# dt from split operands, the context convolution in the first half, a wider-spaced scan, and latent kernels expanded on ScalarE

## The chip, the cores and the metric

One core of a Trainium2 chip runs the whole program as one launch. The metric is the device time of that launch in microseconds (us), lower is better; it is given as the median of repeated runs. The engines are TensorE (PE, with its weight loads PEld), VectorE (DVE), ScalarE (ACT), GpSimd (POOL) and SyncE (SP), which here only issues DMAs. Everything is stored and returned in float32.

## What is computed

One layer of a backbone is applied to 256 context tokens and 2048 latent tokens (a grid of 32 rows by 64 columns), width 1024. Every token is normalised and modulated, projected by one input matrix, passed through two branches, and projected back:

```python
h = rms_norm(x, g_pre) * (1 + scale) + shift
u = h @ w_in
z, xbc, dt_raw, ga, gb, gsil = jnp.split(u, [I_Z, I_XBC, I_DT, I_GA, I_GB], axis=-1)
y_ssd, h_fin = ssd_branch(z, xbc, dt_raw, ...)
y_conf = conformer_branch(ga, gb, ...)        # h = ga*sigmoid(gb); depthwise 31-tap conv; layer_norm; silu
out = jnp.concatenate([y_ssd, y_conf * jax.nn.silu(gsil)], axis=-1) @ w_out
return x + gate * rms_norm(out, g_post), h_fin
```

`ssd_branch` is a Mamba-2 scan in both directions over chunks of 128 tokens: a 5-tap convolution of `xbc`, step sizes `dt = softplus(dt_raw + bias)` (32 columns: 16 heads in two directions), and per chunk a part inside the chunk, a part from the carried state and the new state. In `conformer_branch` the 31 taps run along the context's tokens, and along the rows of the latent grid.

## The kernel before

Tokens are cut into five blocks: block 0 is the context (256 tokens), blocks 1 to 4 are 512 latent tokens each. **Half 0** works on blocks 1, 2, 0, **half 1** on blocks 3 and 4. PSUM has 3 banks for the projections (tag "mm") and 5 for all else (tag "ss").

**Blocks.** `hprep(b)` normalises and modulates a block in eight pieces `ht` of 128 channels and splits each into a high and a low part, `hh` and `hl`, in the type f32r (L283 and L284). A projection runs as three f32r matmuls for each piece, hh·wh (L350), hl·wh (L351), hh·wl (L352): a unit of 24 matmuls fills a bank of 512 tokens. `dt_raw` alone is computed in plain f32, in `split` of `hprep`: one matmul per piece (L282) with 32 weight columns, written to one of four strips of 32 partitions, k % 4. The strips are copied (L300), transposed and added up (L307); `dt_post` makes the scan's factors out of the result.

**Stages.** `xbc_phase` projects `xbc` (banks xp) and starts the 5-tap convolution (`cva`, DVE L447 and L451). `post` then runs 8 `gab_unit`s (banks gb and ga; ACT and DVE make `gth` of them, L501 and L504, which goes to the DRAM buffer `gl`, L505) and 13 or 14 `silu_unit`s (banks sp; `sth`, L514 and L515). In half 0 the scan of chunks 0 to 8 and `gate_rows` run beside `post`, in half 1 the scan of chunks 9 to 17 with `lat_conv` and `ctx_conv`. Last comes the output stage (L1037).

**The scan.** `pass_a(i)` takes one chunk through eleven steps, for two groups g of 8 heads and two directions d. `weigh(g, d)` makes `xw` (DVE L675), its high part `xwh` (ACT L676) and its low part `xwl` (L677, on DVE for d = 1, on POOL for d = 0); `state(g, d)` multiplies them in three matmuls into `pst` (L699, L700, L701); `diag` makes `py`, `off` makes `po`; `carry(g)` puts `po` away as `yo` (DVE L707) and adds `pst` to the running state `Sf` (DVE L709). `state` runs one step after the `weigh` that feeds it, and a new chunk starts each six steps.

**The convolutions.** `ctx_conv(j)` loads 128 channels of the context from `gl` (L549) and runs 31 taps on DVE into the tile `cg` (one L553, 30 L555), then transposes and stores them. `lat_conv(j)` loads the filter rows `kd` and the latent channels `cx`, and four times `expand(u)` writes a block matrix into one of two tiles `kbuf` (L590: 8 copies of 32 partitions x 128, half on DVE, half on ACT), with which PE convolves (banks cp, L601); DVE adds the bias (`cvv`, L606).

**Order.** The generators are stepped against each other by `merge` and `interleave`; a scheduler then orders each engine's instructions by its own estimate, with semaphores between engines. Each engine runs its list in that order. All DMAs are issued by SP, in order.

## Time and profile before

| | |
|---|---|
| median of 3 runs | 1910.53 us (1909.71 to 1910.89) |
| the profiled execution's own time | 1917.09 us |
| its span in the trace | 1915.4 us, mean granted clock 0.986 |
| busy: PE, DVE, ACT, POOL | 1853.9, 1183.0, 786.2, 643.8 us |
| DMA | 375.30 MB, 62.8% of the 16 engines' span |

In time: 0 to 60 us startup, 60 to 200 xbc of half 0, 200 to 770 `post` of half 0, 770 to 950 its last `silu_unit`s, the blocks 3 and 4 and xbc of half 1, 950 to 1460 `post` of half 1, 1460 to the end the output stage. A row of waits names the engine that waits, what for, and the total, the number and the longest. A row of the timeline has start, length, engine, line, operation, tiles and, in brackets, the idle time before it.

### The profile page before, as it was taken

How to read it: one execution, taken by the hardware profiler on the slowest of the kernel's cores; microseconds unless marked ns; L12 is line 12 of the kernel's file. 1: busy time of each engine (PE TensorE's matmuls, PEld its weight loads, DVE VectorE, ACT ScalarE, POOL GpSimd, SP SyncE). 2: the span in 40 equal slices, each digit the busy share in tenths (PEclk: the TensorE clock that was granted, in tenths of full speed). 3: DMA queues.
4: the chain of work that ended last, by engine and by line, in shares of the span. 5: the costliest groups of instructions: out<-in, count | busy, mean ns of one | idle time of the engine just before them, and what ended most of it. 6: DMA issues, size and time to landing. Idle time of an engine off the chain costs nothing.

```text
span 1915.4 us, 27056 instructions
## 1 busy us (share of the span) xinstructions
PE 1853.9 (97%) x9739; PEld 1492.7 (78%) x9739; DVE 1183.0 (62%) x1603; ACT 786.2 (41%) x1746; POOL 643.8 (34%) x612
## 2 busy tenths in 40 slices
PE   7999899999999999999999899989999999999998
PEld 4588778888888878588877667767787888888886
DVE  3687774333344442678597778889437767766752
ACT  3445524444444542346335655555314332222321
POOL 2533423444544432402133343333115322332220
...
GB/s 311 194 189 186 204 220 183 182 219 163 219 218 207 196 230 203 140 160 185 187 180 196 227 238 209 230 216 210 221 264 235 207 165 171 177 172 166 180 99 77
DMA packets 290386, 375.30 MB, mean 196 GB/s; under 512 B 85190, under 2 KB 187462, under 8 KB 290252
## 3 DMA queue, kind: packets, MB, share of 16 engines
q1 hardware_dynamic: 290252, 373.58, 62.8%
...
## 4 chain that ended last, share of the span: by engine, by line
PE 66%; DVE 7%; issue 6%; DMA 3%; POOL 2%; ACT 2%; SPq 0%; POOLq 0%; DVEq 0%
PE op L1037 19%; PE sp L350 6%; PE sp L351 6%; PE sp L352 6%; DVE cg L555 3%; PE xp L350 2%; PE xp L352 2%; PE xp L351 2%; PE gb L350 2%; PE gb L351 2%; PE gb L352 2%; PE ga L350 2%; PE ga L351 2%; PE ga L352 2%; PE qo L944 1%
## 5 line engine op out<-in xcount | busy, mean ns | idle before, releaser
L350 PE MATMUL sp<-hh,wh 128*128 128x512 f32 (+1 forms) x640 | 241.1, 377 | 0.0
L351 PE MATMUL sp<-hl,wh 128*128 128x512 f32 (+1 forms) x640 | 237.3, 371 | 0.0
L352 PE MATMUL sp<-hh,wl 128*128 128x512 f32 (+1 forms) x640 | 236.9, 370 | 0.0
L650 ACT ACTIVATE lb<-lb,WB 128x128 f32<-128x128 f32 x576 | 181.5, 392 | 98.5 <-POOL lb L642 97.1
L350 PE MATMUL xp<-hh,wh 128*128 128x512 f32 (+1 forms) x480 | 181.3, 378 | 8.0 <-ACT raw L435 7.3
L642 POOL TENSOR_SCALAR_AFFINE_SELECT lb<-lb 128x512 f32<-128x512 f32 x144 | 118.9, 833 | 202.3 <-DMA lb<-lt 124.9
L352 PE MATMUL xp<-hh,wl 128*128 128x512 f32 (+1 forms) x480 | 179.6, 375 | 0.6 <-POOL wl L326 0.6
L351 PE MATMUL xp<-hl,wh 128*128 128x512 f32 (+1 forms) x480 | 180.1, 376 | 0.0
L447 DVE SCALAR_TENSOR_TENSOR cva<-raw,cwh,cva 128x1280 f32<-128x1280 f32 (+1 forms) x96 | 154.3, 1612 | 33.5 <-ACT cva L441 31.5
L326 POOL TENSOR_TENSOR wl<-wr,wh 128x512 fp32r<-128x512 f32 x88 | 131.4, 1506 | 122.4 <-ACT wh L325 112.6
L350 PEld LDWEIGHTS sp<-hh,wh 128*128 128x128 f32 x640 | 121.2, 189 | 27.0 <-issue 7.3
L555 DVE SCALAR_TENSOR_TENSOR cg<-cg,cv 128x256 f32<-128x256 f32 x240 | 138.8, 591 | 3.6
L351 PEld LDWEIGHTS sp<-hl,wh 128*128 128x128 f32 x640 | 121.4, 190 | 21.3 <-issue 1.7
L352 PEld LDWEIGHTS sp<-hh,wl 128*128 128x128 f32 x640 | 121.0, 189 | 21.7 <-issue 0.8
L350 PE MATMUL ga<-hh,wh 128*128 128x512 f32 (+1 forms) x320 | 121.3, 379 | 5.8 <-DMA wh<-whd 5.6
L350 PE MATMUL gb<-hh,wh 128*128 128x512 f32 (+1 forms) x320 | 122.3, 382 | 4.5 <-DVE gth L504 4.5
L515 DVE SCALAR_TENSOR_TENSOR sth<-sth,sp 128x512 f32<-128x512 f32 (+1 forms) x80 | 50.3, 631 | 120.8 <-ACT sth L514 116.0
L351 PE MATMUL gb<-hl,wh 128*128 128x512 f32 (+1 forms) x320 | 120.1, 375 | 0.0
L352 PE MATMUL gb<-hh,wl 128*128 128x512 f32 (+1 forms) x320 | 120.0, 375 | 0.0
L351 PE MATMUL ga<-hl,wh 128*128 128x512 f32 (+1 forms) x320 | 119.2, 372 | 0.0
L352 PE MATMUL ga<-hh,wl 128*128 128x512 f32 (+1 forms) x320 | 119.1, 372 | 0.0
L350 PEld LDWEIGHTS xp<-hh,wh 128*128 128x128 f32 x480 | 92.0, 192 | 31.8 <-ACT raw L435 7.9
(218 smaller groups left out, 4033.1 us busy)
## 6 DMA issues: line engine op xcount, KB each, us to landing
lb<-lt SPq DMA_DIRECT2D x144, 256.0 KB, 4.4
wr<-in_w_in SPq DMA_DIRECT2D x88, 256.0 KB, 4.3
...
yp<-yg SPq DMA_DIRECT2D x36, 256.0 KB, 4.4
```

Of the source, the lines that this page charges most:

```text
L326: G.tensor_tensor(wl[:, ks, :], wr, wh[:, ks, :].bitcast(F32), SUB)
L350: T.matmul(ps[:, :BN], wh[:, k, :], hh[:, k, :], start=(k == 0), stop=False)
L351: T.matmul(ps[:, :BN], wh[:, k, :], hl[:, k, :], start=False, stop=False)
L352: T.matmul(ps[:, :BN], wl[:, k, :], hh[:, k, :], start=False, stop=(k == KT - 1))
L447: V.scalar_tensor_tensor(a[:, :n], raw[:, t:t + n], cwh[:, ct * 5 + t:ct * 5 + t + 1], a[:, :n], MUL, ADD)
L515: V.scalar_tensor_tensor(th, th, 1.0, ps[:, :BN], ADD, MUL)
L555: V.scalar_tensor_tensor(acc, g[:, t:t + 256], cv[:, w0 + t:w0 + t + 1], acc, MUL, ADD)
L642: G.affine_select(E[g, hq, d], E[g, hq, d], pattern=[[0, 4], [sg, P]], compare_op=ALU.is_ge, fill=NEG, base=0, channel_multiplier=-sg)
L650: S.activation(lb[:, h, :], lb[:, h, :], AF.Exp, bias=WB[:, i, c + h:c + h + 1])
L944: T.matmul(po[:, q * P:(q + 1) * P], Sb[g][:, q * P:(q + 1) * P], ct[:, g, :], start=True, stop=True)
L1037: T.matmul(pso[n], lhs[:, k % 8, :], w[:, n * 512:(n + 1) * 512], start=(k == 0 and m == 0), stop=(k == 15 and m == 2))
```

## The change

1. **dt.** The f32 matmuls leave `split`. A new generator `dt_block` runs, for each of the eight pieces, two f32r matmuls (L315 with `hh`, L316 with `hl`) with 128 weight columns, of which 32 are the high and 32 the low part of w_dt (the rest belongs to the next piece and is not used); the first two strips are added up. `xbc_phase` steps it between the projections. `w_dt` is split on DVE once.
2. **The context convolution** moves from half 1 to half 0, behind `gate_rows`, takes its tiles from the pool "x4" (three buffers, shared with `gate_rows`), and hands over after every 3 taps rather than 6.
3. **The scan.** `weigh` and `mix` come a step earlier against `diag` and `state`, so `state` runs two steps after its `weigh`; `xwh` and `xwl` have two buffers, `el` is two tiles, and chunks start each seven steps.
4. **The latent kernels** are expanded by 4 ACT copies of 32 x 256 rather than 4 ACT and 4 DVE copies of 32 x 128.
5. `dynamic_dma_scratch_size` is 512 rather than 1024, and one tile of modulation weights is loaded in two DMAs.


```diff
@@ dt: hprep (split), new dt_block, its weights @@
-            q = k % 4
-            T.matmul(pd[q * 32:(q + 1) * 32, :BN], wdt[:, k, :], t, start=(k < 4), stop=(k >= 4))
...
+    def dt_block(b, hb):
...
+        for k in range(KT):
+            w = wdt[:, k * 64:k * 64 + P]
+            T.matmul(pd[:, :BN], w, hh[:, k, :], start=(k == 0), stop=False)
+            T.matmul(pd[:, :BN], w, hl[:, k, :], start=False, stop=(k == KT - 1))
+            if k % 2:
+                yield
...
+    V.tensor_copy(wd4[:, :, 0, :], wdr)
+    V.tensor_tensor(wd4[:, :, 1, :], wdr, wd4[:, :, 0, :].bitcast(F32), SUB)
@@ xbc_phase @@
+                    if s > 10 and s % 2 and dts:
+                        next(dts[0], None)
...
-            if m % (14, 9)[half] == 4:
+            if m % 8 == 4:
                 next(dtp, None)
@@ ctx_conv @@
-        g = lp.tile([P, D], F32, tag="cg", name=f"cg{j}", bufs=2)
+        g = big(f"cg{j}")
...
-            if t % 6 == 0:
+            if t % 3 == 0:
                 yield
@@ lat_conv, expand(u) @@
-                src = kd[rs].rearrange("p r (h u q) -> u p h q r", h=2, u=4)[u]
-                for h in range(2):
-                    eng = S.copy if c4 % 2 else V.tensor_copy
-                    eng(kt[rs, h * 4:(h + 1) * 4, rs], src[:, h])
+                S.copy(kt[rs, :, rs].rearrange("p (h q) r -> p h q r", h=2),
+                       kd[rs].rearrange("p r (h u q) -> p u h q r", h=2, u=4)[:, u])
@@ pass_a: buffers and order of a chunk @@
-            el = pa.tile([P, 8, P], F32, tag="el", name=f"el{i}", bufs=1)
+            for g in range(2):
+                el[g] = pa.tile([P, 4, P], F32, tag=f"el{g}", name=f"el{i}{g}", bufs=1)
...
-            wh = pa.tile([P, 512], F32R, tag="xwh", name=f"xwh{i}{g}{d}", bufs=1)
-            wl = pa.tile([P, 512], F32R, tag="xwl", name=f"xwl{i}{g}{d}", bufs=1)
+            wh = pa.tile([P, 512], F32R, tag="xwh", name=f"xwh{i}{g}{d}", bufs=2)
+            wl = pa.tile([P, 512], F32R, tag="xwl", name=f"xwl{i}{g}{d}", bufs=2)
...
-        diag(0, 0)
-        off(0)
-        state(0, 0)
         weigh(0, 1)
         mix(0, 1)
...
+        diag(0, 0)
+        off(0)
+        state(0, 0)
+        weigh(1, 0)
+        mix(1, 0)
...
         diag(0, 1)
         state(0, 1)
         carry(0)
-        weigh(1, 0)
-        mix(1, 0)
-        decay(1, 1)
+        weigh(1, 1)
+        mix(1, 1)
@@ scan @@
-            if gens and t % 6 == 0:
+            if gens and t % 7 == 0:
@@ main sequence @@
-    interleave(post(0, 6), merge(scan(range(9)), 58, gate_rows(), 9), 90 * 8)
+    extra = chain([gate_rows()] + [ctx_conv(j) for j in range(8)])
+    interleave(post(0, 6), merge(scan(range(9)), 68, extra, 9 + 8 * 13), 90 * 8)
...
-    extra = chain(f for j in range(8) for f in (lat_conv(j, lp, kbuf), ctx_conv(j, lp)))
+    extra = chain([lat_conv(j, lp, kbuf) for j in range(8)])
...
-    interleave(take(blocks, 344), merge(sc_, 54, extra, 8 * 13), 344)
+    interleave(take(blocks, 344), merge(sc_, 63, extra, 8 * 6), 344)
...
-    nc = _bacc.Bacc("TRN2", target_bir_lowering=False, num_devices=1, dynamic_dma_scratch_size=1024)
+    nc = _bacc.Bacc("TRN2", target_bir_lowering=False, num_devices=1, dynamic_dma_scratch_size=512)
```

**PE, dt of block 3** (`pd3` is its bank of dt, `sp0_4640_...` the last silu units of half 0, `xp1_...` the xbc projection of half 1). Before:

```order
L282 MATMUL pd3_6974<-ht3_0_6975,wdt_251 32x512
L350 MATMUL sp0_4640_7_2_7009<-hh2_655,wh5536_0_6748 128x512
L282 MATMUL pd3_6974<-ht3_1_6985,wdt_251 32x512
L351 MATMUL sp0_4640_7_2_7009<-hl2_656,wh5536_0_6748 128x512
L352 MATMUL sp0_4640_7_2_7009<-hh2_655,wl5536_0_6747 128x512
L282 MATMUL pd3_6974<-ht3_2_6998,wdt_251 32x512
L350 MATMUL sp0_4640_7_2_7009<-hh2_655,wh5536_0_6748 128x512
L351 MATMUL sp0_4640_7_2_7009<-hl2_656,wh5536_0_6748 128x512
L352 MATMUL sp0_4640_7_2_7009<-hh2_655,wl5536_0_6747 128x512
L282 MATMUL pd3_6974<-ht3_3_7016,wdt_251 32x512
```

and with the change:

```order
L315 MATMUL pd3_7605<-hh3_7291,wdt_252 128x512
L316 MATMUL pd3_7605<-hl3_7292,wdt_252 128x512
L370 MATMUL xp1_1_3_7583<-hh3_7291,wh1152_1_7252 128x512
L371 MATMUL xp1_1_3_7583<-hl3_7292,wh1152_1_7252 128x512
L372 MATMUL xp1_1_3_7583<-hh3_7291,wl1152_1_7251 128x512
L370 MATMUL xp1_1_3_7583<-hh3_7291,wh1152_1_7252 128x512
L371 MATMUL xp1_1_3_7583<-hl3_7292,wh1152_1_7252 128x512
L372 MATMUL xp1_1_3_7583<-hh3_7291,wl1152_1_7251 128x512
L315 MATMUL pd3_7605<-hh3_7291,wdt_252 128x512
L316 MATMUL pd3_7605<-hl3_7292,wdt_252 128x512
L315 MATMUL pd3_7605<-hh3_7291,wdt_252 128x512
L316 MATMUL pd3_7605<-hl3_7292,wdt_252 128x512
```

The eight f32 matmuls stood one by one among the f32r matmuls of the silu units; sixteen f32r matmuls now stand in pairs and fours among those of the next phase.

**DVE, the taps and `xwl` of chunk 14 in half 1** (`kbuf`, `cvv`: latent convolution; `xwl1401` is the low part for g = 0, d = 1). Before:

```order
L555 SCALAR_TENSOR_TENSOR cg5_11421<-cg5_11421,cv_214 128x256 x2
L590 COPY kbuf1_8122<-kd4_10614 32x4x32
L606 SCALAR_TENSOR_TENSOR cvv4_10624<-cp4_1_10710,cbb4_10611 128x16x32
L590 COPY kbuf1_8122<-kd4_10614 32x4x32 x3
L555 SCALAR_TENSOR_TENSOR cg5_11421<-cg5_11421,cv_214 128x256 x5
L707 TENSOR_TENSOR yo140_10834<-po140_10741,el14_10399 128x512
L555 SCALAR_TENSOR_TENSOR cg5_11421<-cg5_11421,cv_214 128x256
L709 TENSOR_TENSOR Sf0_256<-Sf0_256,pst1400_10746 128x512
L677 TENSOR_TENSOR xwl1401_10752<-xw1401_10750,xwh1401_10751 128x512
```

and with the change:

```order
L701 TENSOR_TENSOR xw1401_10835<-xt140_10721,WS_256 128x512
L631 SCALAR_TENSOR_TENSOR cvv3_10366<-cp3_3_10761,cbb3_10353 128x16x32
L680 TENSOR_TENSOR lb14110_10810<-lb14110_10810,lb14111_10812 128x512
L703 TENSOR_TENSOR xwl1401_10837<-xw1401_10835,xwh1401_10836 128x512
L681 TENSOR_TENSOR lb14110_10810<-lb14110_10810,cb14_10717 128x512
L531 SCALAR_TENSOR_TENSOR gth1_7_3_10700<-gth1_7_3_10700,ga1_7_3_10702 128x512
L701 TENSOR_TENSOR xw1410_10910<-xt141_10790,WS_256 128x512
L733 TENSOR_TENSOR yo140_10944<-po140_10901,el140_10562 128x512
L735 TENSOR_TENSOR Sf0_258<-Sf0_258,pst1400_10906 128x512
```

No tap of the context is left among them, and `xwl1401` stands ahead of the `yo` and `Sf` of its chunk.

**DVE, the gates of half 0** (`gth0_j_b` is gate unit j of block b; `cg2` takes its data from what `gth0_2_0` stored). Before:

```order
L504 SCALAR_TENSOR_TENSOR gth0_2_0_2853<-gth0_2_0_2853,ga0_2_0_2855 128x256
L675 TENSOR_TENSOR xw110_2980<-xt11_2808,WS_254 128x512
L727 TENSOR_TENSOR yg10_2826<-yg10_2826,py10_2868 128x512
L675 TENSOR_TENSOR xw111_3095<-xt11_2808,WS_254 128x512
L504 SCALAR_TENSOR_TENSOR gth0_3_1_3008<-gth0_3_1_3008,ga0_3_1_3010 128x512
L707 TENSOR_TENSOR yo11_3154<-po11_3086,el1_2496 128x512
L709 TENSOR_TENSOR Sf1_257<-Sf1_257,pst110_3091 128x512
L677 TENSOR_TENSOR xwl111_3097<-xw111_3095,xwh111_3096 128x512
```

and with the change:

```order
L531 SCALAR_TENSOR_TENSOR gth0_2_0_3006<-gth0_2_0_3006,ga0_2_0_3008 128x256
L701 TENSOR_TENSOR xw111_3133<-xt11_2890,WS_256 128x512
L680 TENSOR_TENSOR lb2000_3197<-lb2000_3197,lb2001_3199 128x512
L580 TENSOR_SCALAR cg2_3586<-cg2_3586,cv_214,cfb2_249 128x256
L582 SCALAR_TENSOR_TENSOR cg2_3586<-cg2_3586,cv_214 128x256
L753 TENSOR_TENSOR yg10_2908<-yg10_2908,py10_3021 128x512
L582 SCALAR_TENSOR_TENSOR cg2_3586<-cg2_3586,cv_214 128x256 x2
L703 TENSOR_TENSOR xwl111_3135<-xw111_3133,xwh111_3134 128x512
L582 SCALAR_TENSOR_TENSOR cg2_3586<-cg2_3586,cv_214 128x256 x7
L531 SCALAR_TENSOR_TENSOR gth0_3_1_3147<-gth0_3_1_3147,ga0_3_1_3149 128x512
L582 SCALAR_TENSOR_TENSOR cg2_3586<-cg2_3586,cv_214 128x256
L680 TENSOR_TENSOR lb2010_3279<-lb2010_3279,lb2011_3281 128x512
```

Taps now stand between the gates; the first instruction on `cg2` comes three places behind the gate `gth0_2_0` whose stored result it loads. Up to `gth0_3_2` there follow 30 taps, `yg` twice, `lb` five times, and one each of `xwl`, `gth0_3_1`, `yo`, `Sf`, `btl` and `xw`.

## Rows read from the trace of the kernel before

**Rows 1.** The page's first part: busy us and share of the span.
```profile
PE 1853.9 (97%) x9739; PEld 1492.7 (78%) x9739; DVE 1183.0 (62%) x1603; ACT 786.2 (41%) x1746; POOL 643.8 (34%) x612
```

**Rows 2.** What PE waited for: total us, times, longest.
```profile
PE pst L700 <- DVE xwl L677: 15.1, 6, 3.5
PE xp L350 <- ACT raw L435: 7.3, 2, 5.3
PE ga L350 <- DMA wh<-whd: 5.6, 1, 5.6
...
PE cp L601 <- DVE kbuf L590: 3.5, 3, 2.3
...
PE pst L700 <- POOL xwl L677: 1.8, 2, 1.4
```

**Rows 3.** Busy us by stretch: start:end length, PE PEld DVE ACT POOL, PEclk, DMA, GB/s.
```profile
280.00:470.00 190.00, 189.81 (x1076) 158.87 (x1075) 69.42 (x93) 82.97 (x206) 80.84 (x73) 1.00 0.59 194
...
1000.00:1390.00 390.00, 364.64 (x2108) 282.90 (x2109) 306.36 (x538) 206.50 (x536) 131.47 (x136) 0.97 0.81 218
```

**Rows 4.** Slow-clock stretches: one of half 0; of half 1 the first, and five summed.
```profile
272.30:279.10 6.80, 4.27 (x10) 3.40 (x11) 6.40 (x6) 0.00 (x0) 0.64 (x2) 0.50 0.61 227
...
1002.70:1006.10 3.40, 3.40 (x10) 2.69 (x9) 3.40 (x9) 3.40 (x12) 0.42 (x1) 0.50 1.00 185
...
sum 23.80, PE 18.78 PEld 14.88 DVE 19.42 ACT 14.68 POOL 8.76; mean PE 3.76 PEld 2.98 DVE 3.88 ACT 2.94 POOL 1.75
```

**Rows 5.** Groups by line, the dt matmuls: busy us, mean ns, idle before.
```profile
L282 PE MATMUL pd<-ht,wdt 128*32 128x512 f32 (+1 forms) x80 | 33.5, 583 | 1.4 <-ACT ht L291 1.4
```

**Rows 6.** PE's timeline: start of dt's first block; one run of dt matmuls.
```profile
33.72 1.06 PE L282 MATMUL pd<-ht,wdt 128*32 128x512 f32 x1 [1.45 <-ACT ht L291]
...
38.41 0.50 PE L351 MATMUL xp<-hl,wh 128*128 128x512 f32 x1
...
66.24 2.10 PE L282 MATMUL pd<-ht,wdt 128*32 128x512 f32 x8
68.27 0.73 PE L350 MATMUL xp<-hh,wh 128*128 128x512 f32 x2
```

**Rows 7.** PE's timeline: f32r matmuls of 256 and 512 columns in a row.
```profile
105.28 0.28 PE L352 MATMUL xp<-hh,wl 128*128 128x256 f32 x1
105.40 0.40 PE L350 MATMUL xp<-hh,wh 128*128 128x512 f32 x1
105.63 0.40 PE L351 MATMUL xp<-hl,wh 128*128 128x512 f32 x1
```

**Rows 8.** Timelines of DVE and PE around 1115 us.
```profile
1109.46 6.10 DVE L555 SCALAR_TENSOR_TENSOR cg<-cg,cv 128x256 f32<-128x256 f32 x10
...
1117.46 0.68 DVE L677 TENSOR_TENSOR xwl<-xw,xwh 128x512 fp32r<-128x512 f32 x1
...
1118.20 0.50 PE L700 MATMUL pst<-xwl,bth 128*128 128x512 f32 x1 [2.37 <-DVE xwl L677]
```

**Rows 9.** Groups by line on ACT and DVE: busy us, mean ns, idle before.
```profile
L590 ACT COPY kbuf<-kd 32x128 f32<-32x128 f32 x128 | 47.9, 422 | 42.1 <-DMA kd<-in_wconv 33.9 <-PE cp L601 7.3
...
L750 ACT COPY cb<-pb 128x256 f32<-128x256 f32 x18 | 6.6, 369 | 7.9 <-DVE btl L749 7.8
...
L555 DVE SCALAR_TENSOR_TENSOR cg<-cg,cv 128x256 f32<-128x256 f32 x240 | 138.8, 591 | 3.6
```

**Rows 10.** DMA issues, half 0 (first) and half 1: count, KB each, us to landing.
```profile
gl<-gth SPq DMA_DIRECT2D x6, 128.0 KB, 4.7
...
cx<-gl SPq DMA_DIRECT2D x32, 256.0 KB, 6.2
...
cg<-gl SPq DMA_DIRECT2D x8, 128.0 KB, 2.7
```

**Rows 11.** Timelines of DVE and PE at 274 us.
```profile
274.10 0.67 DVE L504 SCALAR_TENSOR_TENSOR gth<-gth,ga 128x512 f32<-128x512 f32 x1
...
274.83 0.80 PE L350 MATMUL gb<-hh,wh 128*128 128x512 f32 x1 [4.45 <-DVE gth L504]
```

More of the change, by code (lines that the diff above doesn't have):

```diff
@@ L184, in backbone_kernel @@
     V.tensor_scalar(cfb2, cv[:, C_CONFB:C_CONFB + 8], 2.0, None, MUL)
-    wdt = pa.tile([P, KT, 32], F32, name="wdt")
+    wdr = pa.tile([P, KT, 32], F32, name="wdr")
+    wdt = pa.tile([P, KT * 64 + 64], F32R, name="wdt")
+    G.memset(wdt[:, KT * 64:].bitcast(F32), 0.0)
     DT = pa.tile([P, HT[0], 32], F32, name="DT")
@@ L209, in modulation @@
             if h == 1 and k in (4, 5):
-                wm = pa.tile([P, 2, 512], F32, tag=("xT", "el")[k - 4], name=f"wm{h}_{k}", bufs=1)
+                wm = None
+                if k == 4:
+                    wm = pa.tile([P, 2, 512], F32, tag="xT", name=f"wm{h}_{k}", bufs=1)
             elif h == 1 and k > 5:
@@ L217, in modulation @@
                 wm = wms[:, k % w]
-            DMA.dma_start(wm, w_mod[k * P:(k + 1) * P, 0:2 * D].rearrange("p (s c) -> p s c", s=2)[:, :, h * 512:(h + 1) * 512])
+            src = w_mod[k * P:(k + 1) * P, 0:2 * D].rearrange("p (s c) -> p s c", s=2)[:, :, h * 512:(h + 1) * 512]
+            if wm is None:
+                wm = [pa.tile([P, 512], F32, tag=f"el{e}", name=f"wm{h}_{k}{e}", bufs=1) for e in range(2)]
+                for e in range(2):
+                    DMA.dma_start(wm[e], src[:, e])
+            else:
+                DMA.dma_start(wm, src)
+                wm = [wm[:, e] for e in range(2)]
             for s in range(4):
-                T.matmul(mp[32 * s:32 * s + 2, 0:256], sc[:, :, k], wm[:, s // 2, s % 2 * 256:s % 2 * 256 + 256],
+                T.matmul(mp[32 * s:32 * s + 2, 0:256], sc[:, :, k], wm[s // 2][:, s % 2 * 256:s % 2 * 256 + 256],
                          start=(k == 0), stop=(k == KT - 1))
@@ L276, in hprep @@
             T.matmul(pr[:, t * P:(t + 1) * P], rs[t].to_broadcast([P, P]), ident, start=True, stop=True)
-        pd = bank("ss", f"pd{b}")
         def split(k):
             t = ts.pop(k)
-            q = k % 4
-            T.matmul(pd[q * 32:(q + 1) * 32, :BN], wdt[:, k, :], t, start=(k < 4), stop=(k >= 4))
             V.tensor_copy(hh[:, k, :], t)
@@ L298, in hprep @@
         yield
+    def dt_block(b, hb):
+        o, BN = TOK[b], BNS[b]
+        nt = BN // P
+        hh, hl = hb[b]
+        pd = bank("ss", f"pd{b}")
+        for k in range(KT):
[4 more added lines that the diff above has]
+                yield
         d4 = ev(f"d4_{b}")
         S.copy(d4[:, :BN], pd[:, :BN])
+        yield
         yield
@@ L358, in dt_post @@
         sl = slice(half * HT[0], half * HT[0] + n)
-        tb = pa.tile([P, D], F32, tag="el", name=f"dtb{half}", bufs=1)
+        tb = pa.tile([P, D], F32, tag="xT", name=f"dtb{half}", bufs=1)
         dt = pa.tile([P, 512], F32, tag="yo", name=f"dtv{half}", bufs=1)[:, 0:n * 32].rearrange("p (i h) -> p i h", h=32)
@@ L463, in xbc_phase @@
         nb = len(ORDER[half])
+        dts = []
         for b in range(nb):
             s = 0
+            dts.append(dt_block(ORDER[half][b], hb))
             for u in first:
@@ L473, in xbc_phase @@
                         next(prep[b], None)
+                    if s > 10 and s % 2 and dts:
+                        next(dts[0], None)
             if b < nb - 1:
                 for _ in prep[b]:
+                    pass
+                for _ in dts.pop(0):
                     pass
@@ L479, in xbc_phase @@
         tail_step()
+        dtp = chain([dts.pop(0), dtp])
         m = 0
@@ L542, in gate_rows, with ctx_conv @@
         yield
-    def ctx_conv(j, lp):
-        g = lp.tile([P, D], F32, tag="cg", name=f"cg{j}", bufs=2)
+    def ctx_conv(j):
+        g = big(f"cg{j}")
         G.memset(g[:, 0:15], 0.0)
@@ L635, in mask @@
             if i != 0:
-                q = 4 * g + 2 * hq
+                q = 2 * hq
                 for j in range(2):
                     rs = slice(j * HD, (j + 1) * HD)
-                    S.activation(el[rs, q:q + 2, :], E[g, hq, 0][rs, j::2, :], AF.Exp)
+                    S.activation(el[g][rs, q:q + 2, :], E[g, hq, 0][rs, j::2, :], AF.Exp)
             for d in range(2):
@@ L730, in close @@
             DMA.dma_start(YP[i][:, g * 512:(g + 1) * 512], y.rearrange("p q l -> p (q l)"))
+        yield
         load_lb(0, 0)
-        yield
         yield
@@ L773, in pass_a @@
         yield
-        diag(0, 1)
-        state(0, 1)
-        carry(0)
+        diag(0, 0)
+        off(0)
+        state(0, 0)
         weigh(1, 0)
@@ L780, in pass_a @@
         yield
+        diag(0, 1)
+        state(0, 1)
+        carry(0)
+        weigh(1, 1)
+        mix(1, 1)
+        yield
         diag(1, 0)
@@ L783, in pass_a @@
         state(1, 0)
-        weigh(1, 1)
         keep(0)
         close(0)
-        mix(1, 1)
         yield
@@ L845, in backbone_kernel @@
     run(modulation(0))
-    DMA.dma_start(wdt.rearrange("p k n -> p (k n)"), w_dt)
+    DMA.dma_start(wdr.rearrange("p k n -> p (k n)"), w_dt)
     for _ in range(4):
```

8 lines of the change are left out of this document (4 added, 4 removed).

## The prediction

> **What bounds the kernel now.** I read the page's first part, then what PE waited for, then busy time by stretch, and last the timelines at the waits. PE is busy 1853.9 of 1915.4 us [rows 1], so only 61.5 us of idle time exist; every other engine is below 62%. A change can gain by taking PE work away, by ending PE's waits, or by raising its clock. The waits are short and of many kinds: the largest, 15.1 us in six, is `state` waiting for the low part `xwl` from DVE; two more of that kind on POOL's `xwl` add 1.8; `kbuf` adds 3.5, a weight load 5.6, ScalarE's `raw` 7.3 [rows 2]. Half 1 is where they lie: of 390 us PE is busy 364.6, with DVE at 306 [rows 3]. There DVE stands 78% full, in half 0 only 37% (69.4 of 190) [rows 3].
>
> What makes `xwl` late can be read at 1115 us: ten taps `cg` hold DVE for 6.10 us, `xwl` starts at 1117.46, and PE's matmul, 2.37 us idle, at 1118.20 [rows 8]. After such waits the granted clock falls to 0.50, the lower of its two levels (1.2 of 2.4 GHz): in half 1 for 23.8 us in five stretches, in which PE was busy 18.78 us [rows 4]. At the full clock that work takes half, so 9.4 us are lost.
>
> **dt.** Removed are 40 f32 matmuls, 80 records, 33.5 us of PE [rows 5]. Added are 16 f32r matmuls for each block: 64 of 512 columns at 0.23 and 16 of 256 at 0.12 us [rows 7], 14.7 + 1.9 = 16.6. The difference is 17 us. Block 1's part before, 33.72 to 38.41 us, lies in the startup, where PE waits for `ht` and modulation weights anyway [rows 6]; those 4.7 us I count as covered. That leaves **-12**. Ends: -17 if that cover is not there, and -2 if the matmuls cost what the best run of them does: eight records, four matmuls, start 2.03 us before the next work [rows 6], 0.51 each, so 32 x 0.51 + 8 x 0.25 = 18 in all. I take the value from the 33.5, which is measured over all of them.
>
> On packing the Trainium skill ("TensorE: Matmul & The Clock Gate", Part 3: Packing small matmuls) states that matmuls in different column tiles run beside each other, 2.38 times as fast for three of 32 columns. The run of four at 0.51 us each agrees in kind, but the order before keeps most of them apart. By the rule for all 40, the 33.5 would be 14, and the change would add 3 us instead of saving 12.
>
> **The scan and the taps in half 1.** With the change no tap is left in half 1's DVE order, and `xwl` stands ahead of its chunk's `yo` and `Sf`, with a whole further step until PE wants it. DVE loses 138.8 of its 306 us there [rows 3, 9]. The waits for `xwl` go: 15.1 + 1.8, **-17**. Nearest ends: all of it, or half, if `xwh`, made on ACT, is late next. `kbuf` leaves DVE: **-3.5**, the three waits [rows 2]. The weight load's 5.6 us wait is of a DMA that SP issues in order; SP loses the 16 DMAs of the taps there, but nothing moves the load itself. I take half, **-3**; ends 0 and -5.6. The clock: most slow stretches follow the waits above, so of 9.4 I take **-8**; ends -5 and -9.4.
>
> **ACT takes the expansion.** 128 copies of 32 x 256 replace 128 of 32 x 128 at 422 ns. Their price has no row: from below a 128 x 256 copy, 369 ns, from above two of the old ones, 844 [rows 9]. At 0.6, nearer the first by its size, ACT gets 25 us more in half 1, of which it uses 206 of 390 [rows 3]; hidden by that margin, and if the margin is gone at one place, PE waits for `kbuf` as it did before, 2.3 at the longest [rows 2]. `lat_conv` is now alone at the end of half 1, where the pieces follow each other closely. I put **+3** for both; ends 0 and +7.
>
> **The taps in half 0.** The work is the same, some 139 us [rows 9], in a half with room. But each piece loads what a gate has just stored. DVE runs in order, and `cg2` stands three places behind its gate `gth0_2_0`: DVE must wait for a store of 128 KB, 4.7 us, and a load, 2.7 [rows 10]. `cg3`, `cg4`, `cg5` stand alike; the other four pieces come long after their gates. What is queued behind is the next gates, and PE waits for those, since a bank is used again three units later. At `cg2`: from the end of unit `ga0_2_0` to the start of `gb0_4_1`, PE has 96 matmuls at 0.23, 48 at 0.12, 9 of `pst` at 0.23 and some 45 short ones of the scan at most at 0.12 [rows 7]: 22.1 + 5.8 + 2.1 + 5 = 35 us. In that time DVE must run `gth0_2_0` (0.4, half of the 0.67 [rows 11] and a little), wait 7.4, run 31 instructions of `cg` at 0.59 [rows 9], 13 others at 0.68 [rows 8] and `gth0_3_2`, 0.67: 0.4 + 7.4 + 18.3 + 8.8 + 0.7 = 35.6. With the issue of two DMAs it is late by about 2 us. Four such places make 8. A PE wait there can cost the clock too: behind the 4.45 us wait at 274 us [rows 11] the clock was 0.50 for 6.8 us with 4.27 us of work [rows 4], a loss of 2.1; for waits half as long I take 1 each. Together **+12**. Ends: 0, and 4 x (4.45 + 2.1) = +26, if each load takes the 6.2 of `cx` [rows 10]. The present wait at 274 us stays, its causes are not touched.
>
> A tap's price is the open term. The Trainium skill ("SBUF — State Buffer", SBUF: two separate sides) states that a VectorE operation with two SBUF inputs and a GpSimd operation shut each other out for a whole instruction. POOL is busy 80.8 of 190 us here against 131.5 of 390 where the 0.59 was measured [rows 3]. If the price went with that share, a tap would cost at most 0.75, 4.7 us more at each of the four places; that would take +12 to about +30.
>
> The split of `el`, the smaller DMA scratch and the two half loads have no row that prices them. I set them at nothing: `el` frees earlier than before, and SP is not what PE waits for but at one load [rows 2]; an upper end is another such wait, +5.6.
>
> **Sum:** -12 - 17 - 3.5 - 3 - 8 + 3 + 12 = -28.5. The profiled execution took 1917.1, 6.6 above the median of the runs, so it would go to about 1888.6; I apply the same difference to the median, 1910.5, and forecast **1882**.
>
> **Rivals.**
> - *Half 0 absorbs the taps* (0.20). DVE is only 37% busy there, and the store may land sooner. Then +12 and +3 go, and the weight load and clock go whole: -12 - 17 - 3.5 - 5.6 - 9.4 = -47.5, **1863**. Against it speaks that DVE cannot overtake a waiting `cg`.
> - *The waits are replaced* (0.17). ACT, with 25 us more, is late with `xwh` or `kbuf`. Then half of the 17, none of the 3.5 and half of the 8 come: -12 - 8.5 - 3 - 4 + 3 + 12 = -12.5, **1898**. For it: ACT runs its list in order, and PE already waited 7.3 us for ACT's `raw` [rows 2]. Against it: a whole step more between `weigh` and `state`.
> - *dt was packed after all* (0.08). If what PE gains is only the 2 us from the price of the best run, the forecast becomes -18.5, **1892**. Against it: busy time of 33.5.
> - *Slower: DVE becomes half 0's bound* (0.09). If all eight pieces wait for their loads, DVE's list falls behind the gates at each gate unit. Eight times 4.45 + 2.1 [rows 4, 11] is +52; with the rest of the change at its weak end, -12 - 17 - 5 + 7 + 52 = +25, **1935**. It turns slower when a piece holds PE, clock loss included, for over about 3.4 us at each of eight places, 27 in all. For it: the calculation above leaves no slack at `cg2`. Against it: four pieces stand late enough behind their gates.
>
> **How the numbers follow.** The forecast case has 0.46 and reaches from 1870 to 1893. The range, **1861 to 1905**, takes in the first three rivals, and the half 0 term at its end of +26 with the weak ends of the weight load, ACT and the clock beside it; outside lie the slower rival and a little of either end. A measurement of this kernel tells about 0.2% (3.8 us) from no change. Faster by more than that: the forecast and the first three rivals less a small part near 1907, **0.86**; within it **0.05**; slower **0.09**.
>
> **What would show it.** Right: no row of PE waiting for `xwl` in half 1; full clock there but for one stretch; dt records near 17 us in all; waits of `gb` for `gth` between 320 and 430 us, with DVE idle for a load of `cg` behind each gate. Wrong: waits of `pst` for `xwh`; no idle of DVE at `cg2` to `cg5`; a gate wait in every unit; PE's busy time down by less than 10 us.

## The result, and the profile after

The changed kernel takes 1901.08 us (median of 7 runs, 1896.96 to 1905.51), the one before 1911.44 in the same comparison: the ratio is 0.9939, with a 95% interval of 0.9919 to 0.9959, about 12 us faster (8 to 15). The forecast was 28.5.

The profiled execution of the changed kernel took 1896.96 us, 4 below its median; the one of before, 1917.09, lay 6 above its own. So the two traces differ by 20 us where the medians differ by 10, and a second profile of the kernel before (1906.4 us, 5 below the median of its own runs, experiment 12) is used to compare stages. The page's first part, of the changed kernel:

```profile
PE 1829.1 (97%) x9739; PEld 1495.8 (79%) x9739; DVE 1167.1 (62%) x1477; ACT 819.3 (43%) x1746; POOL 629.1 (33%) x613
```

PE is busy 24.8 us less than in [rows 1], yet the idle time is 66.1 us, more than the 61.5 of before. What PE waited for, in the changed kernel:

```profile
PE gb L370 <- DVE gth L531: 12.7, 6, 5.8
PE sp L370 <- DVE sth L542: 9.2, 6, 2.6
PE px L688 <- DVE yo L733: 7.5, 4, 4.9
...
PE pdt L325 <- ACT d L320: 2.8, 1, 2.8
...
PE xp L370 <- ACT raw L455: 2.3, 3, 1.0
...
PE pst L725 <- DVE yg L753: 1.8, 1, 1.8
PE cp L626 <- ACT kbuf L614: 1.7, 2, 1.2
```

Nothing waits for DVE's `xwl` any more (15.1 in [rows 2]), and the weight load's wait is gone. In their place stand waits for DVE's gates `gth` and `sth`, 21.9 us in twelve places, all in half 0, and for `yo`. By stretch (start:end length, PE PEld DVE ACT POOL, PEclk, DMA): gate units of half 0, its silu units, gate units of half 1, silu units of half 1, of the second profile of before:

```profile
241.00:505.20 264.20, 263.84 (x1494) 222.61 (x1493) 118.56 (x139) 111.00 (x273) 107.29 (x96) 1.00 0.60 196
505.20:781.60 276.40, 276.40 (x1516) 224.02 (x1515) 118.29 (x172) 120.54 (x286) 113.86 (x110) 1.00 0.62 207
...
924.30:1201.20 276.90, 260.39 (x1511) 202.11 (x1510) 221.75 (x406) 138.10 (x365) 91.67 (x96) 0.98 0.76 207
1201.20:1443.60 242.40, 233.48 (x1272) 186.25 (x1271) 161.62 (x263) 102.05 (x233) 63.58 (x60) 0.98 0.82 234
```

and of the changed kernel:

```profile
227.20:522.40 295.20, 278.96 (x1529) 229.90 (x1528) 240.24 (x353) 116.52 (x287) 116.58 (x113) 0.97 0.56 181
522.40:795.30 272.90, 263.28 (x1477) 220.55 (x1475) 142.56 (x206) 117.66 (x281) 118.77 (x109) 1.00 0.62 206
...
940.20:1198.80 258.60, 249.45 (x1440) 195.90 (x1439) 115.64 (x155) 150.54 (x344) 82.50 (x84) 0.99 0.77 204
1198.80:1434.10 235.30, 232.60 (x1328) 185.65 (x1327) 109.10 (x139) 121.27 (x245) 58.22 (x56) 1.00 0.88 251
```

Half 1 gains 18.3 + 7.1 = 25.4 us. The gate units of half 0 lose 31: DVE's busy time there doubles, from 119 to 240 us, PE goes from idle for 0.4 us to idle for 16, and its clock from 1.00 to 0.97. Against the run without taps (experiment 8: 273.5 us, PE busy 271.0, the same 1529 records) the gate units are 21.7 us longer: 13.8 of them are idle time of PE, 7.9 are matmuls slowed by the lower clock. This first-half loss eats the second half's gain; what is left is dt.

Stage lengths of all kernels follow, read from PE's timeline (first matmul of a kind to the first of the next, us). The output stage is 453.5 to 455.1 in all.

| kernel | median | start and xbc 0 | gates 0 | silu 0 | xbc 1 | gates 1 | silu 1 |
|---|---|---|---|---|---|---|---|
| before, second profile | 1911.7 | 241.0 | 264.2 | 276.4 | 142.6 | 277.0 | 242.4 |
| changed | 1901.1 | 227.2 | 295.2 | 272.9 | 144.8 | 258.6 | 235.3 |
| dt alone | 1890.2 | 230.8 | 264.3 | 267.1 | 142.5 | 281.6 | 240.3 |
| scan alone | 1906.9 | 243.1 | 271.2 | 274.4 | 142.6 | 275.3 | 236.7 |
| taps' move alone | 1913.9 | 239.0 | 294.4 | 287.5 | 142.6 | 248.8 | 232.9 |
| changed, taps back in half 1 | 1885.4 | 226.7 | 275.6 | 265.9 | 146.9 | 265.3 | 239.7 |
| changed, taps beside silu 0 | 1909.3 | 226.3 | 269.7 | 302.4 | 146.2 | 261.6 | 236.0 |
| changed, no taps | 1869.5 | 227.2 | 273.5 | 263.7 | 146.3 | 260.1 | 237.4 |
| changed, half of each piece's taps | 1881.0 | 227.8 | 280.1 | 270.7 | 144.8 | 258.3 | 233.7 |
| changed, half the pieces per half | 1918.4 | 225.9 | 293.7 | 274.1 | 148.3 | 274.3 | 239.4 |
| changed, free stores | 1898.1 | 227.7 | 295.2 | 270.5 | 146.0 | 260.4 | 232.5 |
| changed, old expansion | 1901.9 | 226.2 | 294.8 | 275.1 | 146.5 | 262.2 | 232.7 |
| dt and scan | 1889.3 | 229.6 | 273.1 | 265.1 | 145.9 | 276.9 | 237.6 |
| dt and ACT's expansion | 1880.2 | 230.4 | 265.6 | 267.2 | 142.0 | 274.8 | 236.0 |

### The profile page after: what moved, and what is told of

Same layout as the page of the kernel before. It is cut to its first block, busy times and chain, and to the rows that moved or that the text cites. A ratio compares the mean times of both kernels' runs of the same rounds, so it can differ in the third digit from the quotient of the medians.

```text
span 1895.2 us, 26911 instructions
## 1 busy us (share of the span) xinstructions
PE 1829.1 (97%) x9739; PEld 1495.8 (79%) x9739; DVE 1167.1 (62%) x1477; ACT 819.3 (43%) x1746; POOL 629.1 (33%) x613
## 4 chain that ended last, share of the span: by engine, by line
PE 52%; DMA 12%; DVE 9%; issue 5%; ACT 4%; POOL 3%; SPq 2%; POOLq 0%; DVEq 0%; ACTq 0%
PE op L1068 19%; DMA lb<-lt 6%; PE sp L370 4%; PE sp L371 4%; PE sp L372 4%; DVE cg L582 3%; PE xp L372 2%; PE xp L371 2%; PE xp L370 2%; PE gb L370 2%; ACT lb L676 2%; PE gb L371 2%; PE qo L975 2%; PE gb L372 2%; PE ga L370 1%
## 5 line engine op out<-in xcount | busy, mean ns | idle before, releaser
L668 POOL TENSOR_SCALAR_AFFINE_SELECT lb<-lb 128x512 f32<-128x512 f32 x144 | 106.7, 746 | 296.5 <-DMA lb<-lt 140.1
L582 DVE SCALAR_TENSOR_TENSOR cg<-cg,cv 128x256 f32<-128x256 f32 x240 | 149.5, 626 | 5.5
L370 PEld LDWEIGHTS sp<-hh,wh 128*128 128x128 f32 x640 | 120.6, 188 | 33.5 <-DVE sth L542 11.3
L680 DVE TENSOR_TENSOR lb<-lb,lb 128x512 f32<-128x512 f32 x72 | 62.9, 874 | 116.8 <-ACT lb L676 82.9
```

The source lines that it names most:

```text
L370: T.matmul(ps[:, :BN], wh[:, k, :], hh[:, k, :], start=(k == 0), stop=False)
L582: V.scalar_tensor_tensor(acc, g[:, t:t + 256], cv[:, w0 + t:w0 + t + 1], acc, MUL, ADD)
L668: G.affine_select(E[g, hq, d], E[g, hq, d], pattern=[[0, 4], [sg, P]], compare_op=ALU.is_ge, fill=NEG, base=0, channel_multiplier=-sg)
L680: V.tensor_tensor(a, a, E[g, hq, 1], ADD)
```

## The experiments

**1. The taps back in half 1, all else changed.**

```diff
-    extra = chain([gate_rows()] + [ctx_conv(j) for j in range(8)])
-    interleave(post(0, 6), merge(scan(range(9)), 68, extra, 9 + 8 * 13), 90 * 8)
+    interleave(post(0, 6), merge(scan(range(9)), 68, gate_rows(), 9), 90 * 8)
...
-    extra = chain([lat_conv(j, lp, kbuf) for j in range(8)])
+    extra = chain(f for j in range(8) for f in (lat_conv(j, lp, kbuf), ctx_conv(j, lp)))
```

> The changed kernel with the context convolution put back into half 1 (beside lat_conv, two buffers of its own, handing over each 6 taps); dt, scan and expansion stay changed. In the changed kernel the gate units of half 0 take 295.2 us (first gb to first sp) against 270.6 before, those of half 1 258.6 against 277.8. Theory A, the taps in DVE's list make the gates of half 0 late: gate units of half 0 back to 268 to 273 us and no gb or sp row waiting for gth or sth there beyond 5 us; those of half 1 stay below 267 if the longer way from weigh to state is what ended the xwl waits; total about 1880. Rival B, the new order of the scan makes the gates late: gate units of half 0 stay above 285, total above 1900. Rival C, half 1 gained only because the taps left it: gate units of half 0 near 270, of half 1 back near 275, total about 1890 to 1897.

Measured: 1885.38 us, ratio to before 0.9865 (0.9844 to 0.9885): 16 us faster than the whole change. The gate units of half 0 fall by 19.6 us to 275.6, those of half 1 rise by 6.7, its silu units by 4.4. Theory A comes nearest: with the taps back in it half 1 keeps 14 of its 25 us, and in this kernel moving the taps is a loss. But half 0 stays 3 us and the total 5 us above what A expected.

**2. The taps only beside the silu units of half 0.**

```diff
...
+    units = post(0, 6)
+    interleave(take(units, 48 * 8), merge(sc0, 36, gate_rows(), 9), 48 * 8)
+    interleave(units, merge(sc0, 32, conv, 8 * 13), 42 * 8)
```

> The changed kernel with the context convolution of half 0 stepped only beside the silu units, after all gate units, so that most pieces load what was stored long before. Theory A1, the gates are late because DVE stands in order at the load of what a gate has just stored: gate units of half 0 near 272 us, silu units 268 to 275 us, total 1878 to 1888. Theory A2, it is the taps' time on DVE, wherever they stand: the gain in the gate units comes back as a loss in the silu units, whose stage goes from 273 to 285 us or more with waits of sp for sth of over 15 us; total 1893 to 1902.

Measured: 1909.28 us, ratio 0.9986 (0.9971 to 1.0000). The gate units come down to 269.7, and the silu units go up to 302.4. What PE waited for:

```profile
PE sp L370 <- DVE sth L542: 22.4, 6, 8.1
```

So A2: the loss goes where the taps go, also where most of them load what was stored long before. The total lies 7 us above A2's range.

**3. dt alone.** Of the change only the parts marked dt and `xbc_phase`, with the smaller DMA scratch:

```diff
-            T.matmul(pd[q * 32:(q + 1) * 32, :BN], wdt[:, k, :], t, start=(k < 4), stop=(k >= 4))
...
+            T.matmul(pd[:, :BN], w, hh[:, k, :], start=(k == 0), stop=False)
+            T.matmul(pd[:, :BN], w, hl[:, k, :], start=False, stop=(k == KT - 1))
```

> The kernel before with dt from f32r parts alone (and the smaller DMA scratch). Theory, as predicted: 17 us of PE work less, 12 of them on the path: total 12 us below the kernel before (10 to 17), the xbc stage of half 0 some 10 us shorter than the 206.3 of before, silu units of half 0 some 4 us shorter as block 3's f32 matmuls leave them. Rival, packed strips were cheap already: within 4 us of before.

Measured: 1890.22 us, ratio 0.9901 (0.9877 to 0.9924), 19 us faster (14 to 24), where the theory had 10 to 17. Against the second profile of before, start and xbc of half 0 lose 10.2 us and the silu units 9.3. The groups of its matmuls, by line:

```profile
L306 PE MATMUL pd<-hh,wdt 128*128 128x512 f32 (+1 forms) x40 | 14.7, 372 | 0.0
L307 PE MATMUL pd<-hl,wdt 128*128 128x512 f32 (+1 forms) x40 | 14.6, 370 | 0.0
```

Their busy time of 29 us overlaps that of their neighbours; from their starts to the next matmul's they hold PE for 17.1 us. In the trace of before, the f32 matmuls of blocks 3 and 4 stand alone, and each holds PE for 0.98 us to the next start; two in a row, in different strips, hold it no longer (54.48 us):

```profile
54.48 1.05 PE L282 MATMUL pd<-ht,wdt 128*32 128x512 f32 x4
55.47 0.50 PE L351 MATMUL xp<-hl,wh 128*128 128x512 f32 x1
...
772.16 1.04 PE L282 MATMUL pd<-ht,wdt 128*32 128x512 f32 x2
773.14 0.49 PE L350 MATMUL sp<-hh,wh 128*128 128x512 f32 x1
```

Counted in this way, all 40 hold PE for 29.5 us in the second profile of before, so 12.4 us of the 19 are matmul time: 4.3 in start and xbc of half 0, 7.8 in the silu units. The rest is a wait of PE for ScalarE's copy `raw` near 197 us, in the second profile of before (first line) and here:

```profile
PE xp L350 <- ACT raw L435: 9.3, 2, 8.8
...
PE xp L361 <- ACT raw L446: 3.0, 1, 3.0
```

It is 7.3 to 9.3 us in all four traces with the old dt and 2.1 to 3.0 in all eleven with the new one. The smaller DMA scratch is not the reason: experiment 5 has it too, and waits 9.0 there. The edit also moves the steps of dt's chain among the projections (`m % 8`); which of its lines shortened the wait, no run shows.

The Trainium skill ("TensorE: Matmul & The Clock Gate", Part 3: Packing small matmuls) states that matmuls in different column tiles run beside each other. The pair of the trace agrees, 0.98 us for two as for one, but 28 of the 40 had no such neighbour in PE's order, so little of that speed-up was there to be lost.

**4. The taps' move alone, on the kernel before.**

```diff
-    interleave(post(0, 6), merge(scan(range(9)), 58, gate_rows(), 9), 90 * 8)
+    extra = chain([gate_rows()] + [ctx_conv(j) for j in range(8)])
+    interleave(post(0, 6), merge(scan(range(9)), 58, extra, 9 + 8 * 13), 90 * 8)
...
-    extra = chain(f for j in range(8) for f in (lat_conv(j, lp, kbuf), ctx_conv(j, lp)))
+    extra = chain([lat_conv(j, lp, kbuf) for j in range(8)])
```

> The kernel before with the context convolution moved to half 0 alone (scan, dt and expansion as before). Theory A: gate units of half 0 at 285 to 300 us as in the changed kernel, and half 1 gains because DVE is free there: its gate units 258 to 265 us; total within 8 us of before. Rival B, the scan's new order made half 0 slow: gate units of half 0 below 275 us, total 10 to 20 us below before. Rival D, half 1 needs the longer way from weigh to state: its gate units stay above 272, total 15 to 25 us above before.

Measured: 1913.87 us, ratio 1.0014 (1.0000 to 1.0029). Half 1 gains 28 + 10 us, half 0 loses 30 + 11. The gates are hardly waited for; what PE waited for in the gate units of half 0:

```profile
PE pst L700 <- DVE xwl L677: 9.7, 4, 3.5
PE ga L350 <- ACT gth L501: 3.8, 2, 2.4
PE ga L352 <- POOL wl L326: 2.0, 2, 1.2
```

The `xwl` waits of half 1 have moved into half 0 together with the taps. PE is idle there for 16.5 us, as in the changed kernel (16.2), but mostly for another tile. Theory A holds, in the total (2 us from before) and in half 0; half 1 gains more than it said (248.8 against 258 to 265), so rival D falls: half 1 does not need the longer way from `weigh` to `state`. The gain and the loss cancel.

**5. The scan alone, on the kernel before.** The buffers and the order of a chunk, its start and the steps of the scan, the two half loads and the smaller DMA scratch:

```diff
-            wl = pa.tile([P, 512], F32R, tag="xwl", name=f"xwl{i}{g}{d}", bufs=1)
+            wl = pa.tile([P, 512], F32R, tag="xwl", name=f"xwl{i}{g}{d}", bufs=2)
...
-            if gens and t % 6 == 0:
+            if gens and t % 7 == 0:
...
-    interleave(post(0, 6), merge(scan(range(9)), 58, gate_rows(), 9), 90 * 8)
+    interleave(post(0, 6), merge(scan(range(9)), 68, gate_rows(), 9), 90 * 8)
```

> The kernel before with the scan's part of the change alone (weigh and mix a step earlier, two buffers for xwh and xwl, el in two tiles, chunks seven steps apart); dt, taps and expansion as before, the taps beside lat_conv in half 1. Theory, it is the longer way from weigh to state that ends the xwl waits, not the taps' leaving: the rows of pst waiting for xwl go from 16.9 to under 3 us, gate units of half 1 from 277.8 to 263 to 268 us, total 8 to 15 us below before. Rival, the taps must leave for that: more than 8 us of waits for xwl stay, total within 5 us of before.

Measured: 1906.89 us, ratio 0.9973 (0.9960 to 0.9986), 5 us faster. The waits are the theory's, the total the rival's, and the gate units of half 1 stay at 275.3 where the theory had 263 to 268. No wait for `xwl` is left with all taps in half 1, but others took their place:

```profile
PE px L672 <- DVE yo L717: 7.2, 3, 4.0
PE cp L610 <- DVE kbuf L599: 5.7, 3, 3.4
...
PE pb L747 <- DVE yo L717: 1.8, 1, 1.8
```

`px` and `pb` wait for a bank until DVE has taken `po` away as `yo`: the same DVE, one chunk later. And the gate units of half 0 are 7 us longer than before (271.2), the silu units 2 shorter.

**6. The old expansion in the changed kernel.**

```diff
-                S.copy(kt[rs, :, rs].rearrange("p (h q) r -> p h q r", h=2),
-                       kd[rs].rearrange("p r (h u q) -> p u h q r", h=2, u=4)[:, u])
+                src = kd[rs].rearrange("p r (h u q) -> u p h q r", h=2, u=4)[u]
+                for h in range(2):
+                    eng = S.copy if c4 % 2 else V.tensor_copy
+                    eng(kt[rs, h * 4:(h + 1) * 4, rs], src[:, h])
```

> The changed kernel with the latent kernels expanded as before, half on DVE and half on ACT. Theory, ScalarE's copies cost little either way: within 4 us of the changed kernel (about 1897 to 1905). Rival 1, ACT's copies hold up kbuf and xwh in half 1: 5 us or more faster than the changed kernel. Rival 2, DVE needs the relief in half 1: 5 us or more slower.

Measured: 1901.91 us, ratio 0.9956 (0.9941 to 0.9972): no difference. In the changed kernel a copy takes 657 ns on ACT, near the 0.6 that was taken.

**7. dt and scan, taps and expansion as before.** The edits of experiments 3 and 5 together.

> dt and scan as in the change, context convolution and expansion as before: the two parts that gained or should gain. Theory: their gains add up; dt alone gave about 20 us, the scan about 10, so 1880 to 1886; against the run with ACT's expansion (1885) it shows what the expansion is worth: PE there waited 6.8 us for kbuf on ACT, and if those waits go it is 2 to 6 us faster than that run. Rival: kbuf then waits on DVE behind taps, as long as before (3 to 7 us), and it is within 3 us of that run or slower.

Measured: 1889.34 us, ratio 0.9880 (0.9862 to 0.9898), where dt alone gave 1890.22: the gains do not add up, and the rival holds (4 us slower than experiment 1). PE waited for `kbuf` on DVE:

```profile
PE cp L628 <- DVE kbuf L617: 7.7, 5, 3.6
PE px L690 <- DVE yo L735: 6.4, 3, 2.7
```

**8. No taps.** The 30 later taps are left out, the loads and the first instruction behind them stay.

```diff
-            V.scalar_tensor_tensor(acc, g[:, t:t + 256], cv[:, w0 + t:w0 + t + 1], acc, MUL, ADD)
             if t % 3 == 0:
                 yield
```

> The changed kernel without 30 of the 31 taps of the context convolution in half 0 (this part of the result is left out); the loads behind the gates, the first instruction that waits for them, the transposes and stores stay. Theory A1, standing in order at the loads is what makes the gates late: gate units of half 0 stay above 284 us (changed: 295.2) and gb keeps more than 6 us of waits for gth. Theory A2, it is the time of the taps themselves in DVE's list: gate units at 264 to 274 us, under 3 us of such waits, sth waits of half 0 under 2 us, total 1868 to 1882.

Measured: 1869.45 us, ratio 0.9786 (0.9770 to 0.9803). The gate units take 273.5 us, DVE's busy time in them is 133.4, and the clock is back at 1.00:

```profile
227.20:500.70 273.50, 271.04 (x1529) 225.66 (x1528) 133.40 (x159) 117.94 (x289) 111.69 (x115) 1.00 0.60 199
```

A2 again: DVE still stands 21.0 us at the loads, and the gate units are as short as in experiment 7 (273.1), which has neither taps nor loads there. Standing at the loads alone costs nothing that can be seen; 150 us of taps cost 32.

**9. Four pieces in each half.**

```diff
-    extra = chain([gate_rows()] + [ctx_conv(j) for j in range(8)])
+    extra = chain([gate_rows()] + [ctx_conv(j) for j in range(4)])
...
+    extra = chain(f for j in range(8) for f in ([lat_conv(j, lp, kbuf)] + ([ctx_conv(4 + j // 2, lp)] if j % 2 else [])))
```

> The changed kernel with the context convolution shared out: channels 0 to 3 beside all of half 0, channels 4 to 7 beside the latent convolution of half 1. Without taps the changed kernel takes 1869, with all of them in half 0 1901 (32 more), with all in half 1 1885 (16 more). Theory Q, what costs is dense runs of taps ahead of work that PE waits for, so a thinner stream costs less than its share: 1872 to 1883, gate units of half 0 at 268 to 277 us, fewer than 5 us of gb waiting for gth, half 1 like the run without taps within 4 us. Rival L, every tap costs its share where it stands: half of 32 and half of 16 on 1869 gives 1893.

Measured: 1918.43 us, ratio 1.0039 (1.0025 to 1.0053), slower than either theory and than both kernels. The four pieces of half 0 did not thin out: all 120 of their taps run before 520 us, in longer runs. At 345 us, timeline of DVE and SP, then DVE and PE:

```profile
345.98 6.44 DVE L582 SCALAR_TENSOR_TENSOR cg<-cg,cv 128x256 f32<-128x256 f32 x10
352.33 0.68 DVE L531 SCALAR_TENSOR_TENSOR gth<-gth,ga 128x512 f32<-128x512 f32 x1
...
353.04 0.32 SPq L532 DMA_DIRECT2D gl<-gth  x1
353.64 0.83 SPq L656 DMA_DIRECT2D lb<-lt  x2
...
361.94 0.69 DVE L680 TENSOR_TENSOR lb<-lb,lb 128x512 f32<-128x512 f32 x1 [7.13 <-ACT lb L676]
...
369.14 0.42 DVE L775 TENSOR_TENSOR btl<-pb,bth 128x256 fp32r<-128x256 f32 x1 [5.91 <-ACT bth L774]
...
370.24 0.68 DVE L531 SCALAR_TENSOR_TENSOR gth<-gth,ga 128x512 f32<-128x512 f32 x1
...
370.98 0.79 PE L370 MATMUL gb<-hh,wh 128*128 128x512 f32 x1 [5.02 <-DVE gth L531]
```

Ten taps hold a gate; SP's store of it is late, and the mask loads `lb` behind the store with it; through POOL and ACT that comes back to DVE, which stands 7.13 us for `lb` and 5.91 more for ACT's `bth`, with the next gate behind both in its list. PE then waits 5.02. In half 1 PE waited 15.9 us for ACT's `kbuf`. Why half of the pieces cost as much as all, this run doesn't tell.

**10. dt and ACT's expansion, scan and taps as before.** The edit of experiment 3 and, against the kernel before, the one of experiment 6 the other way round.

> dt from parts and the expansion on ScalarE; scan and taps as before. dt alone gave 1890, with scan and expansion 1885, with scan alone 1889. Theory, the scan's new order only exchanges waits, and ACT's expansion frees DVE in half 1: 1882 to 1888, with xwl waits of pst still near 10 us. Rival, the scan's order is what the 1885 needs: 1888 to 1895.

Measured: **1880.17 us**, ratio 0.9842 (0.9827 to 0.9858), 30 us faster than before and 21 than the changed kernel: the fastest of the kernels here that compute everything, 2 us below the theory's range. `xwl` waits remain, less than the 12.6 us of the second profile of before, with the new scan left out:

```profile
PE pst L716 <- DVE xwl L693: 6.2, 6, 2.2
```

ACT's expansion, worth nothing where the taps are in half 0 (experiment 6), is worth 10 us over dt alone where the taps share DVE with it.

**11. Free stores.** The 16 stores of latent gates in half 0 take a weight tile as their data, so the latent channels are left out of the result.

```diff
-            DMA.dma_start(GL[j][:, o:o + BN], th)
+            src = wa[0][:, 0:4, :].rearrange("p k n -> p (k n)").bitcast(F32) if half == 0 and b else th
+            DMA.dma_start(GL[j][:, o:o + BN], src)
```

> The changed kernel in which the 16 stores of half 0's latent gates take their data from a weight tile instead of the gate (the latent channels that the convolution of half 1 reads are left out of the result); the same bytes go to the same place, but SP no longer stands in order at a store until DVE has made the gate. In the changed kernel SP waited 72.4 us at these stores between 227 and 520 us (35.7 without taps), and the loads of the scan's masks lb stand behind them. Theory S, a chain from late gates over SP to late masks and back to DVE is what makes taps dear in half 0: gate units go from 295.2 to 275 to 285 us, total 1880 to 1891. Rival D, DVE's list is simply too full: gate units stay above 289 us, total 1895 or more.

Measured: 1898.07 us, ratio 0.9925 (0.9909 to 0.9941), gate units unchanged at 295.2. SP's waits, 227 to 520 us:

```profile
SPq L657 <- DVE lb L681: 69.1, 13, 12.3
SPq L533 <- DVE gth L531: 21.3, 4, 11.2
```

The wait at the stores fell from 72.4 to 21.3, and SP stood instead at the mask loads themselves, 69.1 us (47.9 in the changed kernel), until DVE had done with the tile to be overwritten. Theory S falls and rival D's numbers hold: taking the store's wait away moved it one instruction on.

**12. The kernel before, again.** No edit.

> The kernel before, unchanged, for a second profile: the first one took 1917.1, 5.7 above the median of its runs by now. Theory V1, the difference lies in the waits in half 1 and at raw (scattered stages), the output stage stays within 1 us of 453.7. Theory V2, it lies in one place: one stage differs by over 4 us.

Measured: 1911.69 us, ratio 0.9999 (0.9988 to 1.0010), its profile 1906.4. The gate units take 264.2 us here and 270.6 in the first profile, every other stage agrees within 1.7: V2. The first profile's wait at 274 us [rows 11] and the slow clock behind it [rows 4] belong to that one execution.

**13. Half of the taps in each piece.**

```diff
         for t in range(1, CW):
-            V.scalar_tensor_tensor(acc, g[:, t:t + 256], cv[:, w0 + t:w0 + t + 1], acc, MUL, ADD)
+          if t % 2:
+            V.scalar_tensor_tensor(acc, g[:, t:t + 256], cv[:, w0 + t:w0 + t + 1], acc, MUL, ADD)
```

> The changed kernel with 15 of the 30 later taps in every piece (the other taps are left out of the result): all eight pieces, their loads and their places stay, the time of taps on DVE in half 0 is half. With all taps 1901, with none 1869. Theory N, the taps cost only once DVE's list is behind the gates: 1869 to 1880, gate units 270 to 279 us. Rival L, each tap costs its share: 1882 to 1888, gate units near 284.

Measured: 1881.01 us, ratio 0.9834 (0.9816 to 0.9851), and gate units of 280.1, between the two: the first half of the taps costs 12 us, the second 20. In these two steps the price of a tap rises with the load on DVE, but the first half is not free either.

## Why the prediction was wrong

**The bound and the waits: right, the size partly by luck.** PE was the bound, the `xwl` waits went, and in half 1 the stages lost 25.4 us where the terms -17, -3.5, -3, -8 and +3 make -28.5. `kbuf` waits fell to 1.7, the slow clock in half 1 nearly went (0.98 to 0.99 and 1.00). But the cause given was half right. Experiment 5 shows that the longer way from `weigh` to `state` ends these waits alone, and gains only 7.4 us in half 1, as other waits come in their place; experiment 4 shows that the taps' leaving alone takes half 1 to 248.8 + 232.9, 37.7 us less than before. Both together gain 12 us less than that. The expansion is not the reason (experiment 6: 262.2 + 232.7); in half 1 PE waits 5.1 us for `yo` in the changed kernel and not at all in experiment 4. The new scan is the likeliest cause, but dt and the taps' move without it were not run together.

**dt: right for the matmuls, short by a wait.** The term was -12; the part measured -19 (14 to 24). The matmuls alone come to 29.5 - 17.1 = 12.4 by their starts (experiment 3), so -12 stands, though in part by luck: the 33.5 us of busy time counts overlaps, and the 4.7 us taken off for block 1 happened to make up for it. What was put at nothing is the wait for `raw`, named in [rows 2] with 7.3 us but not in the sum: it went from 9.3 to 3.0 us, and that is most of what the term lacks.

**The taps in half 0: the step that failed.** The term was +12, with an end of +26; the taps cost 32 (experiment 8), 31 of them in the gate and silu units. The working looked at one place, `cg2`, let DVE begin there with an empty list, put a load wait of 7.4 us into its sum, and took the four places alike. In the changed kernel PE ends `ga0_2_0` at 327.7 us, but DVE comes to its gate only at 337.59, 10 us late, behind taps of the piece before; the load of `cg2` is then waited for 1.22 us only. DVE's timeline before the longest gate wait, and PE's:

```profile
337.59 0.41 DVE L531 SCALAR_TENSOR_TENSOR gth<-gth,ga 128x256 f32<-128x256 f32 x1
...
339.30 1.80 DVE L680 TENSOR_TENSOR lb<-lb,lb 128x512 f32<-128x512 f32 x1
342.32 0.41 DVE L580 TENSOR_SCALAR cg<-cg,cv,cfb 128x256 f32<-128x256 f32 x1 [1.22 <-DMA cg<-gl]
...
358.73 4.38 DVE L582 SCALAR_TENSOR_TENSOR cg<-cg,cv 128x256 f32<-128x256 f32 x8
...
367.54 3.80 DVE L681 TENSOR_TENSOR lb<-lb,cb 128x512 f32<-128x512 f32 x3
371.26 1.48 DVE L582 SCALAR_TENSOR_TENSOR cg<-cg,cv 128x256 f32<-128x256 f32 x1
372.67 0.68 DVE L531 SCALAR_TENSOR_TENSOR gth<-gth,ga 128x512 f32<-128x512 f32 x1
...
373.39 0.79 PE L370 MATMUL gb<-hh,wh 128*128 128x512 f32 x1 [5.82 <-DVE gth L531]
```

Between the first instruction on `cg2` and the gate DVE waits for next to nothing (0.1 us); three `lb` take 3.80 us where 0.68 each was put, and a tap takes 0.626 us in the mean, not 0.591, so the tap's own price, the open term, was a small part. This is the place of the forecast (35.6 against 35 us, "late by about 2"), late by 5.8. And it is not one of four: `gth` and `sth` are waited for in twelve places of both stages. The load waits were there, in other places than `cg2` and unlike each other; what DVE waited for at the loads in the gate units (total us, times, longest):

```profile
DVE cg L580 <- DMA cg<-gl: 18.1, 5, 11.0
```

But experiment 8 has them too (21.0 us), and its gate units are none the longer for them. The rival "DVE becomes half 0's bound", at 0.09, had the mechanism (taps ahead of gates in an in-order list) and too steep a price, 52 us; what it gave as cause, the loads, was not it by themselves.

**The scan in half 0: not in the sum.** The new order of the scan makes the gate units there longer (271.2 in experiment 5, 273.1 in experiment 7, against 264.2), partly scan work that moved forward from the silu units, by some 5 us net. Nothing in the prediction priced it.

**The sum.** By the second profile of before: start and xbc -13.8, half 0's units +27.5, xbc of half 1 +2.2 (PE waits 2.8 us for ACT's copy `d`, since dt now ends there), half 1 -25.4: -9.5, near the 10.4 of the medians. "The waits are replaced" (1898) came nearest in time, by luck: the replacement was by DVE, not by ACT. That 1901 lies within the range is luck in part too: the taps cost more than their end of +26, and dt gave more than its term.

Open stays why DVE is waited for in half 0 when it is busy 81% of the gate units: experiment 9 shows a circle through four lists in order (DVE, SP, POOL, ACT, and DVE again), experiment 11 that cutting it at one point doesn't help. Whether a shorter run of taps between two gates would help was not tried.
